# Weights stored as contiguous tiles, parameters in one pack, natural channel order, and the second gate's blocks moved into the mixers

## The chip, the cores and the metric

The kernel runs on one core of one Trainium2 chip. The metric is the device time of one execution in microseconds (us). Before the change three runs took 1486.04, 1483.69 and 1480.70 us, a median of 1483.69 us. A difference of about 0.3% (4.4 us) is what a measurement of this kernel can tell from no change.

## What is computed

A trunk of two layers over 256 tokens of 1024 channels in fp32, batch 1, with a conditioning vector c:

```python
cond = jax.nn.silu(c)
for l in range(DEPTH):
    mod = cond @ w_ada[l] + b_ada[l]
    shift1, scale1, gate1, shift2, scale2, gate2 = [m[:, None, :] for m in jnp.split(mod, 6, axis=-1)]
    h = rms_norm(x, norm1_g[l]) * (1 + scale1) + shift1
    proj = h @ w_in[l] + b_in[l]
    mq, mk, mv, mo, mgates, aq, ak, av, gm, ga = jnp.split(proj, offsets, axis=-1)
    y_m = mlstm_mixer(...)            # depthwise convolution of 5 taps on q and k, then a gated recurrence
    y_a = bidirectional_gqa(...)      # attention with q/k norms and rotary embedding
    merged = sigmoid(gm) * (y_m @ w_branch_m[l]) + sigmoid(ga) * (y_a @ w_branch_a[l])
    x = x + gate1 * (merged @ w_out[l])
    h2 = rms_norm(x, norm2_g[l]) * (1 + scale2) + shift2
    x = x + gate2 * hierarchical_moe(h2, ...)   # top group of 4, top 2 of its 8 experts, 32 experts of SwiGLU
return rms_norm(x, final_norm_g)
```

Nearly all the bytes are weights. Per layer `w_ada` has 25.2 MB, `w_in` 20 MB, `w_branch_m` and `w_branch_a` 2.1 MB each, `w_out` 4.2 MB, and the 32 experts 201.3 MB.

## The kernel before, in words

**One stream of weight tiles.** A list `plan` holds every weight tile in the order of use, a tile being 128 partitions of 2048 fp32 numbers, 1.049 MB. `pump()` (L156-173) walks through it: as long as a place is free that fits the next tile, SyncE (SP) issues its DMA (L172). `wt()` hands a tile to the arithmetic, and `done()` gives its place back. The places are 16 slots of an arena, of which 0, 1, 2 and 15 (`BASE`) always serve and the others only while their other contents are dead, three tiles "y", two tiles "x" (only while the experts run) and, in the mixer only, one tile "z" ("spare" in the profile). An expert tile never goes to "z". Since SP issues in the order of the plan, a tile that has no place holds back all that are behind it.

**The mixer** (`mixer`, one call per layer) computes everything up to `x + gate1 * ...`. Each weight tile is split on chip into a rounded part and a rest (`prep`, L532-547: a cast on ScalarE at L537, a subtraction at L518 on VectorE for one half and GpSimd for the other) and multiplied in three passes; a quarter of a 512-column pair of tiles is one `dense` step, 24 matmuls of TensorE (PE) that take about 3.1 us. The string `MIX[l]` is the order of the rest around these steps: a digit is a number of dense steps, a name is a piece of other work. `gates` and `gates2` make the recurrence's gates; `dec0` to `dec4` (L788-834) make its decays by short alternations of PE, VectorE and ScalarE; `r5` to `r9` and `r4` are blocks of 512 columns of the layer's own `w_ada`, `c0` to `c3` blocks of the next layer's. Each block has two tiles (`ada_sums`, L423-431), a round over ScalarE and VectorE (`ada_part`) and a pair of matmuls (`ada_sum`, "prow"). q and k go through the convolution in `fin_qk` (L605-615): one ScalarE copy with bias, one VectorE `tensor_scalar` (L611), four `scalar_tensor_tensor` (L613), one ScalarE silu.

**The end of the mixer.** After `MIX` come the two branch products, the output projection `wo` with `fin_wo` (L1094-1107), which writes x, the scaled copy `xa` (slot 5) and the same numbers in another channel order, `xaP` (slot 6), and the router's logits. The blocks 10 and 11 of `w_ada` (`GATES`, the second gate) stand in the plan behind `wo` and ahead of the experts' tiles. `ada_sums` of both runs on PE when the logits are done (L1153), and their sums are folded into `gt2b` in the first pair of experts (L1461-1463, L1482-1487, "prow").

**The experts** (`experts`) run 16 pairs. Per pair: 4 tiles of gate, 4 of up, 4 of down; the product act_mul (L1337), its transposes (L1343), their copy (L1344), the down product, and a scatter back into x. Behind pair 11 (`MIDDLE`) the program tests whether an expert has more than 64 rows (`rest`).

**Places at that moment.** When the second gate's blocks are on PE, the stream has the arena's 0, 1, 2, 15, then 8, 11, 12 (released at L1078) and 7, 13, 14 (`free:7:13:14` in `MIX`), and the three "y" (L1130): 13 places. The two "x" are released at the start of `experts` (L1169), and 4, 5 and 6 after the first one-hot (L1458): 18 in all.

**Weights in HBM** are the reference's arrays. A `w_ada`, `w_in`, `w_branch` or `w_out` tile is read in rows of 2 KB; an expert tile in rows of 8 KB, 16 KB apart. The small parameters come in some 20 DMAs: `params` (L317-351) reads rows that PE transposes (`params_cols`, L353-358), for layer 1 in its experts' pair 6; the router is read in both channel orders.

Of the kernel before, what the change touches and what calls it, by code (L numbers as in the profile page):

```python
# [54 lines left out]


def trunk(ctx, tc, x, c, w_ada, b_ada, norm1_g, w_in, b_in, conv_w, conv_b, mlstm_norm_g, q_norm_g, k_norm_g,
          w_branch_m, w_branch_a, w_out, norm2_g, w_rg, b_rg, w_re, b_re, w_gate, w_up, w_down, final_g,
          rope, out, dbg=None, depth=DEPTH):
# [183 lines left out]
    def first_params():  # L243
        first["p"] = params(0, nc.gpsimd, nc.sync)

    for l in range(depth):
# [5 lines left out]
        for it in stream(l):  # L252
            if it[0] in DENSE:
                o = DENSE[it[0]] + 512 * it[1]
                src = w_in[l].rearrange("(k p) c -> p k c", p=P)
# [1331 lines left out]
```

## Time and profile before

| what | us |
|---|---|
| median of three runs | 1483.69 |
| the profiled execution's own time | 1483.02 |
| its span, first to last instruction | 1481.1 |
| PE busy, of the span | 1345.1 (91%) |
| VectorE (DVE) busy | 630.1 (43%) |
| ScalarE (ACT) busy | 399.4 (27%) |
| GpSimd (POOL) busy | 281.2 (19%) |

521.5 MB move in the span. The profile's page gives the span in 40 slices of 37 us, with a row of the DMA rate in GB/s. The view of windows gives, for stretches of one's choice, each engine's busy time with its number of instructions, then the granted clock of PE as a share of full speed, the busy share of the 16 DMA engines (small overshoots over 1 are its rounding), and GB/s. The timeline gives start, duration, engine, line, operation, written and read tile and shape, and in brackets the idle time ahead of it with who ended it; on SP a row such as "x4" covers four issues with the waits between them. The mixer of layer 0 lies between 0 and 282 us, its experts between 282 and 757, the mixer of layer 1 up to 996, its experts up to the end.

### The profile page before, as it was taken

The numbers are of one execution on the slowest core, as the hardware profiler recorded it, in microseconds if no ns is written. First come the engines' busy times: TensorE is split into PE (matmuls) and PEld (weight loads), VectorE is DVE, ScalarE is ACT, GpSimd is POOL, SyncE is SP. The second block draws the span as 40 slices with busy tenths as digits, with TensorE's granted clock in tenths as the row PEclk, the third lists the DMA queues.
The fourth block names the chain that finished last, engine by engine and source line by source line (L and its number), as shares of the span: only waits on it lengthen the run. The fifth ranks groups of instructions, "written<-read, shape, count | busy, mean of one in ns | idle before, by whom it ended". The sixth has DMA issues, their size and how long they took to land. (4 is left out here: it accounts for less than half of the span.)

```text
span 1481.1 us, 20274 instructions
## 1 busy us (share of the span) xinstructions
PE 1345.1 (91%) x7870; PEld 782.3 (53%) x7871; DVE 630.1 (43%) x1390; ACT 399.4 (27%) x749; POOL 281.2 (19%) x321
## 2 busy tenths in 40 slices
PE   5899999899999989879889899998999989988996
PEld 2887789734434434234348788983443443434332
DVE  2786666613323313223258776664232332213223
ACT  2535564511101101001045367552110110101101
POOL 3645336300000000000025543550000000000000
PEclk8899999999999999999999999999999999999998
DMA  9956698699999999999997537659999999999995
GB/s 323 357 212 210 228 340 289 245 422 421 420 421 421 421 421 421 421 413 380 405 388 254 198 130 260 232 223 398 421 420 422 421 420 421 421 422 419 370 421 230
DMA packets 124248, 521.50 MB, mean 352 GB/s; under 512 B 15924, under 2 KB 18176, under 8 KB 76016
## 3 DMA queue, kind: packets, MB, share of 16 engines
q1 hardware_dynamic: 118064, 516.11, 87.7%
q0 software_dynamic: 1200, 2.13, 0.6%
q10 hardware_dynamic: 4880, 1.87, 0.5%
q8 instruction: 65, 1.06, 0.3%
q14 instruction: 39, 0.32, 0.1%
HBM read 519.03 MB, written 1.05 MB: 351 GB/s over the span
## 5 line engine op out<-in xcount | busy, mean ns | idle before, releaser
L1328 PE MATMUL pgu<-arena 128*64 128x512 f32 x1520 | 418.6, 594 | 17.7 <-DMA arena<-in_w_up_dram 14.0
L1328 PEld LDWEIGHTS pgu<-arena 128*64 128x64 f32 x1520 | 138.1, 137 | 235.7 <-issue 179.4
L1337 DVE SCALAR_TENSOR_TENSOR arena<-pgu,wsl,arena 128x512 f32<-128x512 f32 x32 | 36.4, 1136 | 391.8 <-PE pgu L1328 391.8
L1353 PE MATMUL pd<-arena 128*64 128x512 f32 x640 | 179.6, 601 | 10.8 <-ACT arena L1344 10.8
L1284 POOL TENSOR_TENSOR arena<-oh,arena 128x256 f32<-128x256 f32 x32 | 19.5, 615 | 733.0 <-DVE oh L1278 474.4
L596 PE MATMUL pd<-R,R 128*128 128x256 f32 x1056 | 139.7, 291 | 9.8 <-DVE R L518 5.5
L577 PE MATMUL pd<-R,R 128*128 128x256 f32 x1008 | 134.5, 292 | 8.3 <-ACT R L537 4.3
L596 PEld LDWEIGHTS pd<-R,R 128*128 128x128 f32 x1056 | 132.6, 196 | 14.9 <-DVE R L518 6.3
L577 PEld LDWEIGHTS pd<-R,R 128*128 128x128 f32 x1008 | 127.4, 197 | 17.2 <-ACT R L537 5.3
L1364 DVE TENSOR_TENSOR y<-pd,arena 128x512 f32<-128x512 f32 x64 | 44.1, 691 | 204.3 <-PE pd L1353 169.3
L518 POOL TENSOR_TENSOR R<-arena,R 128x512 fp32r<-128x512 f32 (+1 forms) x73 | 108.4, 1486 | 104.0 <-ACT R L537 80.3
L1328 PE MATMUL pgu<-X,arena 128*64 128x512 f32 x240 | 106.6, 594 | 6.4 <-DMA X<-in_w_up_dram 6.4
L1365 ACT CAST yh<-y 128x512 fp32r<-128x512 f32 x64 | 39.6, 619 | 241.7 <-DVE y L1364 241.7
L518 DVE TENSOR_TENSOR R<-arena,R 128x512 fp32r<-128x512 f32 (+1 forms) x81 | 75.8, 945 | 59.1 <-ACT R L537 49.7
L1353 PEld LDWEIGHTS pd<-arena 128*64 128x64 f32 x640 | 54.7, 138 | 87.1 <-issue 72.1
L1328 PE MATMUL pgu<-B,arena 128*64 128x512 f32 x288 | 87.1, 595 | 7.2 <-DMA B<-in_w_gate_dram 5.9
L1376 DVE TENSOR_TENSOR xs<-xs,psc 128x512 f32<-128x512 f32 x128 | 79.3, 679 | 19.0 <-PE psc L1373 19.0
L1300 PE MATMUL pG<-oh,X 128*128 128x256 f32 x512 | 70.6, 298 | 13.0 <-DVE oh L1278 12.0
L537 ACT CAST R<-arena 128x1024 fp32r<-128x1024 f32 x65 | 67.8, 1045 | 51.5 <-PE pd L596 15.5
L1300 PEld LDWEIGHTS pG<-oh,X 128*128 128x128 f32 x512 | 67.0, 204 | 24.1 <-issue 22.6
L1344 ACT COPY arena<-pat 128x512 f32<-128x512 f32 x32 | 18.7, 585 | 222.5 <-PE pat L1343 222.5
L1353 PE MATMUL pd<-B,arena 128*64 128x512 f32 x240 | 70.8, 595 | 3.6 <-ACT arena L1344 3.6
(346 smaller groups left out, 1708.9 us busy)
## 6 DMA issues: line engine op xcount, KB each, us to landing
arena<-in_w_up_dram SPq DMA_DIRECT2D x100, 1024.0 KB, 19.8
arena<-in_w_gate_dram SPq DMA_DIRECT2D x90, 1024.0 KB, 19.8
arena<-in_w_down_dram SPq DMA_DIRECT2D x80, 1024.0 KB, 19.8
arena<-in_w_ada_dram SPq DMA_DIRECT2D x35, 1024.0 KB, 7.7
B<-in_w_down_dram SPq DMA_DIRECT2D x30, 1024.0 KB, 19.8
arena<-in_w_in_dram SPq DMA_DIRECT2D x22, 1024.0 KB, 7.9
X<-in_w_gate_dram SPq DMA_DIRECT2D x20, 1024.0 KB, 19.8
B<-in_w_gate_dram SPq DMA_DIRECT2D x18, 1024.0 KB, 19.8
```

The lines of the kernel that those rows point to most:

```text
L518: eng.tensor_tensor(dst, full, hi.bitcast(F32), op=ALU.subtract)
L537: A.copy(wh, w)
L577: T.matmul(acc[key][o][:, 0:S], lhsT=w[:, kk, P * o:P * o + P], rhs=x_[:, 4 * kh + kk], start=kh == 0 and i == 0 and kk == 0, stop=kh == 1 ...
L596: T.matmul(acc[key][t][:, 0:256], lhsT=x_[:, 4 * kh + kk, P * t:P * t + P], rhs=w[:, kk], start=kh == 0 and i == 0 and kk == 0, stop=kh == ...
L1284: G.tensor_tensor(ow, oh[:, :, 2 * (i % 2):2 * (i % 2) + 2].bitcast(F32), cb[:, :, 2 * i:2 * i + 2].unsqueeze(3).to_broadcast([P, NT, 2, C ...
L1300: T.matmul(pG[:, kk, 0:n], lhsT=x_[:, t, k, :], rhs=oh[:, t, :], start=i == 0, stop=i == 3)
L1328: T.matmul(pg[CAP * e:CAP * e + CAP, :], lhsT=xg[4 * h + kk][:, P * (i % 2) + CAP * e:P * (i % 2) + CAP * e + CAP], rhs=w[e][:, kk, :], st ...
L1337: V.scalar_tensor_tensor(ac.rearrange("p k q -> p q k"), pu.rearrange("p (q k) -> p q k", k=4), wsl[:, 0:1], sl.rearrange("p (q k) -> p q ...
L1353: T.matmul(pd[n][CAP * e:CAP * e + CAP, :], lhsT=aT[:, 2 * h + kk, CAP * e:CAP * e + CAP], rhs=w[e][:, kk, 512 * n:512 * n + 512], start=h ...
L1364: V.tensor_tensor(y[:, cs], pd, gt2b[:, cs], op=ALU.mult)
L1365: A.copy(yh[:, cs], y[:, cs])
L1376: V.tensor_tensor(xx, xx, pq, op=ALU.add)
```

## The change

**Layouts.** The host writes each weight tile as one contiguous block of 1 MB (`ada_t`, `in_t`, `branch_t`, `out_t`, `gate_t`, `up_t`, `down_t`), so every tile is read in rows of 8 KB; only the last pair's down tiles stay at 2 KB. The small parameters of a layer are one array `packs[l]` of 128 x 540 numbers, already as columns, read by one DMA: for layer 0 on ScalarE's queue, for layer 1 on GpSimd's. The router is one array, read once per layer by GpSimd, in natural order.

**Natural channel order.** `xaP` and its eight copies per layer go; `experts` reads `xa`. Slot 6 is released with the "y" places instead of after the first one-hot. `shift_put` makes 4 matmuls instead of 8. act_mul writes a contiguous tile instead of one with a stride.

**Second gate.** `GATES` is gone: the blocks 10 and 11 are `r10` and `r11` in `MIX`, with `ada_part` and `ada_row` like the others, in both layers.

**Order.** In `MIX` the decays start behind the convolution: `dec0` stands six (layer 0) and six (layer 1) dense steps behind `gates2`. The convolution's first tap goes from VectorE to ScalarE.

```diff
-    "1 tables 1 gates 2 gates2 dec0 4 dec1 1 dec2 2 dec3 1 dec4 1 kr 2 1 kt qr:0 2 qr:1 r6 1 hold ...
+    "1 tables 1 gates 2 gates2 6 dec0 2 dec1 1 kr 1 dec2 1 dec3 r10 1 kt qr:0 1 dec4 1 qr:1 r6 1 hold ...
...
-            s = w_ada[l].rearrange("(p k) c -> p k c", k=KD)[:, 4 * h:4 * h + 4, 512 * b:512 * b + 512]
-            add(("ada", l, b, h), s, (4, 512))
+            add(("ada", l, b, h), ada_t[l, b, h].rearrange("p (k c) -> p k c", k=4), (4, 512))
...
-        for b in GATES:
-            plan_ada(l, b)
...
+    def params(l, q):
+        pk = sm.tile([P, NPK], F32, tag="pk", name="pk", bufs=1)
+        q.dma_start(pk, packs[l])
+        p = {nm: pk[:, o:o + n] for nm, (o, n) in PK.items()}
...
-            V.tensor_scalar(a, pre[:, 0:S], cols[:, 32 + j:33 + j], cols[:, 72 + j:73 + j], op0=ALU.mult, op1=ALU.add)
+            A.activation(a, pre[:, 0:S], AF.Identity, scale=cols[:, 32 + j:33 + j], bias=cols[:, 72 + j:73 + j])
...
-            dst = xaP[:, t, :, 32 * n:32 * n + 32].rearrange("p k q -> p q k")
-            if n == 3:
-                G.tensor_tensor(dst, xs[:, t, cs].rearrange("p (q k) -> p q k", k=KD),
-                                A2b[:, cs].rearrange("p (q k) -> p q k", k=KD), op=ALU.mult)
-            else:
-                A.copy(dst, xa[:, t, cs].rearrange("p (q k) -> p q k", k=KD))
...
-        release([("y", s) for s in range(3)])
+        release([("y", s) for s in range(3)] + [("a", 6)])
...
-        gates_ = [ada_sums(l, b) for b in GATES]
...
-            V.scalar_tensor_tensor(ac.rearrange("p k q -> p q k"), pu.rearrange("p (q k) -> p q k", k=4), wsl[:, 0:1],
-                                   sl.rearrange("p (q k) -> p q k", k=4), op0=ALU.mult, op1=ALU.mult)
+            V.scalar_tensor_tensor(ac.rearrange("p k q -> p (k q)"), pu, wsl[:, 0:1], sl, op0=ALU.mult, op1=ALU.mult)
...
-        release([("a", 4), ("a", 5), ("a", 6)])
+        release([("a", 4), ("a", 5)])
...
-                for h, s in enumerate(sums):
-                    pc = ps.tile([P, 512], F32, tag="f", name="prow")
-                    T.matmul(pc, lhsT=ones, rhs=s, start=True, stop=True)
...
-            if not last and i == 6:
-                params_cols(nextp)
```

**SP, the end of layer 0's mixer.** These are the DMAs from the output projection's weights on, before and then after; "B" are the "y" places and "X" the "x" places. Before:

```order
L172 DMA arena<-in_w_out_dram 128x4x512 x4
L172 DMA arena<-in_w_ada_dram 128x4x512 x4
L172 DMA arena<-in_w_gate_dram 128x2048 x2
L172 DMA B_2571<-in_w_gate_dram 128x2048
L172 DMA B_2572<-in_w_gate_dram 128x2048
L172 DMA B_2573<-in_w_up_dram 128x2048
L172 DMA arena<-in_w_up_dram 128x2048 x3
L172 DMA arena<-in_w_down_dram 128x2048 x4
L172 DMA arena<-in_w_gate_dram 128x2048
L172 DMA X_2929<-in_w_gate_dram 128x2048
```

After:

```order
L176 DMA arena<-in_out_t_dram 128x2048 x4
L176 DMA arena<-in_gate_t_dram 128x2048 x4
L176 DMA arena<-in_up_t_dram 128x2048 x2
L176 DMA B_2572<-in_up_t_dram 128x2048
L176 DMA B_2573<-in_up_t_dram 128x2048
L176 DMA B_2574<-in_down_t_dram 128x2048
L176 DMA arena<-in_down_t_dram 128x2048 x3
L176 DMA arena<-in_gate_t_dram 128x2048 x2
L176 DMA X_2901<-in_gate_t_dram 128x2048
```

The four blocks of `w_ada` between `wo` and the experts' tiles are gone, and 14 instead of 13 experts' tiles are issued ahead of the first "X", of which all 14 have a place that does not depend on the second gate's matmuls.

**VectorE, the output projection of layer 0.** "lc" is the router's offset, "R" the split weights, L1097 (L1046 after) the first operation of `fin_wo`. Before:

```order
L1136 TENSOR_TENSOR lc<-pL,br 128x36
L518 TENSOR_TENSOR R_146<-arena,R_146 128x512
L518 TENSOR_TENSOR R_145<-arena,R_144 128x256
L518 TENSOR_TENSOR R_147<-arena,R_147 128x512
L1097 TENSOR_TENSOR arena<-pd,arena 128x256 x2
```

After:

```order
L1079 TENSOR_TENSOR lc<-pL,pk 128x36
L471 TENSOR_TENSOR R_141<-arena,R_141 128x512
L471 TENSOR_TENSOR R_140<-arena,R_139 128x256
L471 TENSOR_TENSOR R_142<-arena,R_142 128x512
L696 TENSOR_TENSOR c1b<-c_726,pk 128x16
L665 SCALAR_TENSOR_TENSOR A_5315<-c1b,pk 128x8
L1046 TENSOR_TENSOR arena<-pd,arena 128x256 x2
```

Two small operations of layer 1 (its `c1` and `A1`, L696 and L665 of the changed kernel) now stand in the middle of layer 0's output projection. The first of them reads "pk", layer 1's pack, whose DMA GpSimd can issue only after "lc" has read layer 0's pack, since there is one buffer. Before, `c1` of layer 1 stood in the experts, behind the transposed parameters.

**PE, the end of layer 0's mixer.** "pL" are the logits, "pada" the blocks of `w_ada`, "pp" the routing's counts, "pG" the gather. Before:

```order
L1141 MATMUL pL<-arena 128x36 x4
L428 MATMUL pada<-arena,condp 32x512 x16
L1238 LDWEIGHTS trisb
L1238 MATMUL pp<-arena,trisb 128x64
L1239 LDWEIGHTS onesb
L1239 MATMUL pp<-arena,onesb 128x32
```

After:

```order
L1084 MATMUL pL<-arena 128x36 x4
L1180 LDWEIGHTS trisb
L1180 MATMUL pp<-arena,trisb 128x64
L1181 LDWEIGHTS onesb
L1181 MATMUL pp<-arena,onesb 128x32
```

The 16 matmuls of the second gate between the last logits and the counts are gone from this place and stand earlier, in two groups of 8 between dense steps.

More of the change, by code (lines that the diff above doesn't have):

```diff
@@ L243, in first_params @@
     def first_params():
-        first["p"] = params(0, nc.gpsimd, nc.sync)
+        first["p"] = params(0, nc.scalar)
     for l in range(depth):
@@ L445, in ada_fast, with columns @@
         return t
-    def ada_shift(l, b):
-        A.copy(turned_sums, ada_sums(l, b).rearrange("p (q k) -> p k q", k=KD))
-    def shift_put(sh2c, b3, b):
-        o = 64 * (b % 2)
-        pc = ps.tile([P, 512], F32, tag="f", name="pshift")
-        for k in range(KD):
-            T.matmul(pc[o:o + 64, 2 * k:2 * k + 2], lhsT=turned_sums[:, k, :], rhs=ones[:, 0:2], start=True, stop=True,
-                     tile_position=(0, o))
-        V.tensor_tensor(sh2c[o:o + 64, :], pc[o:o + 64, 0:2 * KD].rearrange("p (k o) -> p k o", o=2)[:, :, 0],
-                        b3[o:o + 64, :], op=ALU.add)
-    def ada_put(c1, cols, b, t):
+    def columns(t):
         pc = ps.tile([P, 512], F32, tag="f", name="pcol")
@@ L464, in ada_put, with ada_shift, shift_put @@
             T.matmul(pc[:, 2 * j:2 * j + 2], lhsT=t[:, P * j:P * j + P], rhs=ones[:, 0:2], start=True, stop=True)
-        V.tensor_tensor(c1[:, 4 * b:4 * b + 4], pc[:, 0:8].rearrange("p (j o) -> p j o", o=2)[:, :, 0],
-                        cols[:, 80 + 4 * b:84 + 4 * b], op=ALU.add)
+        return pc[:, 0:8].rearrange("p (j o) -> p j o", o=2)[:, :, 0]
+    def ada_shift(l, b):
+        A.copy(sums_at, ada_sums(l, b))
+    def shift_put(sh2c, b3, b):
+        s = slice(4 * (b % 2), 4 * (b % 2) + 4)
+        V.tensor_tensor(sh2c[:, s], columns(sums_at), b3[:, s], op=ALU.add)
+    def ada_put(c1, cols, b, t):
+        V.tensor_tensor(c1[:, 4 * b:4 * b + 4], columns(t), cols[:, 80 + 4 * b:84 + 4 * b], op=ALU.add)
     def ada_sum(parts):
@@ L1172, in experts @@
         pump()
-        xp = [t.rearrange("p (t k q) -> p t k q", t=NT, k=KD) for t in tiles["x"][2:4]]
+        xp = [t.rearrange("p (t c) -> p t c", t=NT) for t in tiles["x"][2:4]]
         used = [1024]
@@ L1455, in experts @@
         with tc.issue_after(marks["oh"].ins):
-            marks["lo"] = V.scalar_tensor_tensor(xp[1][:, 1], xaP[:, 1], r, xp[0][:, 1].bitcast(F32), op0=ALU.mult,
+            marks["lo"] = V.scalar_tensor_tensor(xp[1][:, 1], xa[:, 1], r, xp[0][:, 1].bitcast(F32), op0=ALU.mult,
                                                  op1=ALU.subtract)
-        release([("a", 4), ("a", 5), ("a", 6)])
+        release([("a", 4), ("a", 5)])
         gather(oh)
         urgent.close()
-        sums = [at(9, 512 * i, 512) for i in range(2)]
-        for s, pb in zip(sums, gates_):
-            A.copy(s, pb)
         with tc.issue_after(marks["lo"].ins):
```

157 lines of the change are left out of this document (71 added, 86 removed).

## The prediction

> **What bounds the kernel now.** I read the page's row of DMA rates first, since nearly all of the work is weights. Slices are 37 us.
>
> ```profile
> GB/s 323 357 212 210 228 340 289 245 422 421 420 421 421 421 421 421 421 413 380 405 388 254 198 130 260 232 223 398 421 420 422 421 420 421 421 422 419 370 421 230
> ```
>
> Two plateaus at 420 to 422 GB/s, the experts, and between them mixers at half of that. Two questions follow: does the stream or PE set the plateaus, and when do they begin? The view of windows (PE, PEld, DVE, ACT, POOL busy, then clock, DMA share, GB/s):
>
> ```profile
> 20.00:24.00 4.00, 3.20 (x28) 2.02 (x24) 1.85 (x7) 1.37 (x3) 1.39 (x3) 1.00 1.05 383
> 64.00:68.00 4.00, 4.00 (x21) 4.00 (x20) 1.02 (x2) 3.96 (x7) 1.78 (x1) 0.50 1.05 389
> 280.00:284.00 4.00, 3.24 (x30) 1.90 (x34) 3.79 (x21) 2.92 (x6) 0.89 (x1) 1.00 0.00 0
> 292.00:296.00 4.00, 4.00 (x25) 3.74 (x26) 2.29 (x11) 1.42 (x3) 0.00 (x0) 0.72 1.01 422
> 300.00:304.00 4.00, 4.00 (x17) 1.40 (x14) 0.14 (x1) 0.10 (x1) 0.00 (x0) 1.00 1.01 422
> 1000.00:1004.00 4.00, 2.94 (x28) 0.68 (x20) 3.36 (x20) 1.83 (x3) 0.00 (x0) 0.90 0.92 285
> 40.00:120.00 80.00, 71.47 (x544) 63.70 (x546) 62.19 (x158) 33.50 (x47) 44.92 (x60) 0.91 0.78 277
> 760.00:880.00 120.00, 108.34 (x852) 93.48 (x845) 92.49 (x237) 62.00 (x101) 62.45 (x71) 0.97 0.64 226
> ```
>
> At 280 the stream stands still; from 292 the DMA engines are full. An expert tile (1.049 MB) takes 1.049/0.422 = 2.49 us, a pair of 12 tiles 29.8 us. What PE needs for a pair is read from the copy that stands once in each pair (timeline of ScalarE):
>
> ```profile
> 313.90 0.58 ACT L1344 COPY arena<-pat 128x512 f32<-128x512 f32 x1 [8.11 <-PE pat L1343]
> ...
> 368.36 0.58 ACT L1344 COPY arena<-pat 128x512 f32<-128x512 f32 x1 [9.34 <-PE pat L1343]
> ...
> 421.11 0.58 ACT L1344 COPY arena<-pat 128x512 f32<-128x512 f32 x1 [9.34 <-PE pat L1343]
> ...
> 745.29 0.58 ACT L1344 COPY arena<-pat 128x512 f32<-128x512 f32 x1 [11.29 <-PE pat L1343]
> ...
> 1027.64 0.58 ACT L1344 COPY arena<-pat 128x512 f32<-128x512 f32 x1 [8.11 <-PE pat L1343]
> ```
>
> Two pairs took 421.11 - 368.36 = 52.75 us while tiles lay ready, 26.4 a pair. Fifteen took 745.29 - 313.90 = 431.4 where PE alone would need 396: some 35 us in which PE waited for tiles. So an experts' phase ends at the start of its full stream plus its remaining bytes, and tiles that have landed before the stream must wait are worth 2.49 us each. How many have landed is counted on SP's timeline:
>
> ```profile
> 231.93 10.98 SPq L172 DMA_DIRECT2D arena<-in_w_gate_dram  x2
> 249.03 0.80 SPq L172 DMA_DIRECT2D B<-in_w_gate_dram  x2
> 249.88 0.42 SPq L172 DMA_DIRECT2D B<-in_w_up_dram  x1
> 256.82 14.65 SPq L172 DMA_DIRECT2D arena<-in_w_up_dram  x3
> 273.58 11.70 SPq L172 DMA_DIRECT2D arena<-in_w_down_dram  x4
> ...
> 286.18 0.95 SPq L172 DMA_DIRECT2D X<-in_w_gate_dram  x2
> ```
>
> Of the last four-fold row the first went out at 273.58, the others had to wait until the second gate's tiles were read. So 2 + 2 + 1 + 3 + 1 = 9 tiles lay ready at 280, and the full stream runs from about 286. In layer 1 the window at 1000 moved 1.14 MB, 2.7 us at 422, so it starts near 1001.
>
> The mixers are another matter: in the two stretches from 40 and from 760 PE idles 8.5 and 11.7 us, VectorE is busy for 78%, and the clock (0.91, 0.97) costs PE another 6.4 and 3.3 us.
>
> **Start of layer 0.** Eight blocks of `w_ada` and x, 9.44 MB, must come ahead of the first dense step (PE's timeline):
>
> ```profile
> 30.31 1.93 PE L428 MATMUL pada<-arena,condp 128*32 128x512 f32 x8 [0.69 <-DMA arena<-in_w_ada_dram]
> ...
> 38.20 10.41 PE L577 MATMUL pd<-R,R 128*128 128x256 f32 x72 [2.45 <-ACT R L537]
> ```
>
> Up to 30.31 PE waits for a DMA. Rows of 2 KB went at 383 and 389 GB/s with the engines full, the experts' 8 KB rows at 422. After, 9.72 MB with the pack at 422 take 23.0 us, and with a head of 3 us (estimated: 9.44 MB at 383 would be 24.6, and the small loads stand between) the last tile lands at 26.0: -4.3. Bounds: the rate alone, 24.6 to 23.0, about -2; and -6 if the head goes with the small loads.
>
> By the Trainium skill ("DMA: Bandwidth & Descriptors", Specifications) a transfer is at line rate from 512 B on, so rows of 2 KB would lose nothing. The trace differs, 383 against 422 GB/s with full engines; by the page the term would be nil and the sum 1474.3.
>
> **Mixers.** Off VectorE goes the first tap, eight times in the stretch (groups of lines, mean ns behind the busy time):
>
> ```profile
> L611 DVE TENSOR_SCALAR arena<-arena,cols 128x256 f32<-128x256 f32 x8 | 3.2, 409 | 2.3 <-ACT arena L609 2.1
> ```
>
> That is 3.2 us a layer for an engine that PE waits for; ScalarE, which takes it, is busy for 42% of the stretch. The decays, short turns between three engines, leave the convolution's VectorE queue. Both together can take no more than the idle 8.5 and 11.7 us plus the clock's loss, and no less than nothing; I take -6 a layer, about twice the taps and half the idle time, a choice. Against that stand two rows r10 and r11 between dense steps. Their price (PE's timeline, first the 4 tiles of both blocks, then a pair of row sums):
>
> ```profile
> 282.10 3.64 PE L428 MATMUL pada<-arena,condp 128*32 128x512 f32 x32
> 287.78 0.20 PE L1238 MATMUL pp<-arena,trisb 128*128 128x64 bf16 x1 [2.04 <-DVE arena L1235]
> ...
> 290.52 5.23 PE L1300 MATMUL pG<-oh,X 128*128 128x256 f32 x29 [0.51 <-DVE X L1456]
> 295.68 3.65 PE L1328 MATMUL pgu<-arena 128*64 128x512 f32 x16
> ```
>
> ```profile
> 218.61 0.62 PE L471 MATMUL prow<-part,onesr 128*128 128x512 f32 x2
> ```
>
> 3.64 + 2 x 0.62 = +4.9 a layer, all of it on PE's path in the mixer. At the mixer's end it saves nothing: PE waited there for the routing (L1238 begins at 287.78 behind VectorE's L1235), and the 3.64 us lay in front of that. Net -1 a layer, -2 in all; bounds +10 (no relief) and -15. The copies `xaP` go from ScalarE and GpSimd, which did not end a wait there: zero.
>
> **PE cold at the end.** Without those matmuls PE is idle from 282.1 to 287.8, 5.7 us. The clock is already 0.72 in the window at 292, where the gather and the first gate matmuls run. I take +1 a layer, +2 in all; bounds nil, as it is low anyway, and +4, if the 5.23 us of the gather went at the 0.50 that the window at 64 shows instead of 0.72 (5.23 x 0.72/0.50 = 7.5).
>
> The Trainium skill ("TensorE: Matmul & The Clock Gate", Part 1) lets PE fall to half rate after an idle window of some 3.4 us; by that the gather would lose up to 1.7 us a layer and the sum would be 1.4 us more. The trace's 0.72, behind only 2.0 us of idle time, shows that the clock falls there without such a window too.
>
> **A new wait: layer 1's pack.** In VectorE's order `c1` of layer 1 (L696) now stands in layer 0's output projection. It needs layer 1's pack, which GpSimd can issue only after "lc", as there is one buffer. The nearest rows are the router's bias, which GpSimd issues at that place, and the two operations between which L696 would stand (timelines of GpSimd and VectorE, then DMA issues with KB and us to landing):
>
> ```profile
> 253.79 0.56 POOL L329 DMA_DIRECT2D br<-in_b_router_group_dram  x1
> ```
>
> ```profile
> 256.68 0.74 DVE L1097 TENSOR_TENSOR arena<-pd,arena 128x256 f32<-128x256 f32 x2
> 257.34 1.27 DVE L518 TENSOR_TENSOR R<-arena,R 128x512 fp32r<-128x512 f32 x1
> ```
>
> ```profile
> br<-in_b_router_group_dram POOLq DMA_DIRECT2D x1, 2.0 KB, 6.7
> br<-in_b_router_expert_dram POOLq DMA_DIRECT2D x1, 16.0 KB, 8.1
> ```
>
> So the pack (276 KB) lands between 253.8 + 6.7 = 260.5 and 262, and VectorE stands from 256.7 on. Behind L696 on its queue are `fin_wo`'s L1097 (L1046 now) and the split L518 (L471 now) of the next weights, which PE needs here:
>
> ```profile
> 260.81 3.11 PE L596 MATMUL pd<-R,R 128*128 128x256 f32 x24
> ```
>
> L518 would run from 261.2 to 262.7 or from 262.7 to 264.2 instead of ending at 258.6, with L1097 ahead of it. PE is late by 2 to 4 us, and the logits, which hang on `fin_wo`, by up to 5. I take +5, as the pack is 17 times the larger of the two loads; bounds +1 and +9. Layer 1 has no next pack.
>
> **Places of tiles.** After the change the second gate holds none of the arena's places at the mixer's end, and slot 6 serves earlier: 14 places, then the two "x" and slots 4 and 5, 18 in all. The first place comes back when the first gate half is done, 295.68 + 3.65 = 299.3, its new data some 2 us later, 301.5. By then 9 + (301.5 - 286) / 2.49 = 15.2 tiles have landed now, and 18 will have: a full ring, so the gain is 2.8 tiles, 7.0 us, and not the five tiles (12.4 us) of 14 against 9. In layer 1 the same point lies at 301.5 + (1027.64 - 313.90) = 1015.2, with 9.5 + 14.2 / 2.49 = 15.2 tiles landed (9 as in layer 0, and half a tile more by estimate, since what goes before 1001 isn't counted), and the gain is some 6.7 us. Together -13.7; bounds nil, if the mixer ends with places still unread, and -25.
>
> The rate in the experts' phases stays at 422: both kernels read those tiles in 8 KB rows. act_mul's straight tile lies under the stream: zero.
>
> **Sum.** -4.3 - 2 + 2 + 5 - 13.7 = -13.0, from the profiled execution's 1483.0 (0.7 under the median): **1470.0**.
>
> **Rivals.**
> *The relief is whole.* Both mixers lose all idle time (20.2) and half of the clock's loss (4.8), less 9.8 of added rows: -15.2 instead of -2, and the pack has landed in time: 1470.0 - 13.2 - 5 = 1451.8. For it speaks VectorE's 78%; against it that half of the idle time can have other causes.
> *Contiguous experts' tiles stream faster by 1%.* 945 us of stream in both layers make -9.4: 1460.6. Against it: the share is 1.01 already.
> *Rows of 2 KB were at line rate.* The start gives nothing: 1474.3, the page's rule from above.
> *The ring gains nothing.* The tiles ready are read no sooner, since the ring is full either way by the time PE takes the first: 1483.7.
> *The added rows wait for tiles (slower).* In the mixer r10 and r11 add four tiles to a stream that is busy for 78% from 40 to 120 and has few places there. If PE waits for both tiles of each of the four rows, 2 x 2.74 us at 383 GB/s, 22 us come on top: 1492. It decides from 4.4 us a row on (17.4 us in all); against it speaks that the blocks r5 to r9 come through that stretch already and VectorE, not the stream, is what is busiest beside PE there.
>
> **How the numbers follow.** Forecast 0.52, whole relief 0.14, faster stream 0.10, start without gain 0.08, ring without gain 0.09, waiting rows 0.07. About 0.3%, 4.4 us, is what a measurement of this kernel can tell from no change, so "same" is 1479.3 to 1488.1. The forecast's own terms scatter by some 7 us, so 0.05 of its 0.52 lies in it, with 0.06 of the full ring and 0.01 of the waiting rows: 0.12. Slower: 0.06 of the waiting rows and 0.01 of the full ring. Faster: 0.81. The range reaches from the whole relief, 1450, to the ring without gain, 1484.
>
> **What would show it.** Right: the DMA's first slice above 323 GB/s and dense steps from 34 on; no window at 0 GB/s ahead of the experts; a VectorE stall on "pk" in layer 0's output projection; copy L1344's successors 7 us earlier after the mixer's own shift; clock below 0.72 at the gather. Wrong: PE waiting on `w_ada` tiles between dense steps; stretches 40 to 120 and 760 to 880 with more PE idle time than 8.5 and 11.7; a plateau above 424 GB/s; "pk" landing before VectorE asks for it.

## The result, and the profile after

Six runs of the changed kernel took 1472.08 to 1475.85 us, median 1472.8, against 1485.09 for six of the kernel before: ratio 0.9927, interval 0.9911 to 0.9943, so 0.6 to 0.9% faster. The profiled execution took 1472.51 us, its span 1470.4, 10.7 less than before. The forecast was 1470.0, 13.0 less.

The page's row of DMA rates after, in slices of 37 us:

```profile
GB/s 383 368 257 238 253 366 276 205 367 419 419 420 419 420 420 419 420 393 399 413 411 258 241 175 233 233 261 294 420 419 419 420 419 419 420 419 418 372 420 236
```

The first slice has risen from 323 to 383. The slices at the start of the plateaus have fallen (367, and 294 in layer 1), which looks like a loss and isn't: there the ring, that is all the places for tiles, is full. And the plateau itself is at 419 to 420 where it was 421 to 422.

The first dense step (timeline of PE):

```profile
32.12 10.24 PE L530 MATMUL pd<-R,R 128*128 128x256 f32 x72 [2.45 <-ACT R L490]
```

It comes 6.1 us earlier than before (38.20). The last tile of `w_ada` that it needs is multiplied from 26.73 on where it was 30.31, 3.6 us earlier. The other 2.5 us lie behind that tile, where PE ran at a granted clock of 0.50 before and of 0.97 to 1.00 now: its 8 matmuls took 1.93 us and take 1.07, the 16 that follow took 3.57 and take 1.95 (before, then after; timeline and window of PE):

```profile
32.18 3.57 PE L464 MATMUL pcol<-onesr,arena 128*128 128x2 f32 x16
28.00:32.00 4.00, 3.31 (x16) 0.20 (x8) 0.00 (x0) 0.00 (x0) 0.00 (x0) 0.50 1.05 387
```

```profile
26.73 1.07 PE L385 MATMUL pada<-arena,condp 128*32 128x512 f32 x8 [0.57 <-DMA arena<-in_ada_t_dram]
27.73 1.95 PE L408 MATMUL pcol<-onesr,arena 128*128 128x2 f32 x16
28.00:32.00 4.00, 1.67 (x15) 1.59 (x15) 2.38 (x8) 1.85 (x4) 0.34 (x4) 0.97 1.00 410
```

The two mixers, each from its first dense step to the output projection, before and then after, in the view of windows:

```profile
38.20:250.53 212.33, 202.84 (x1606) 177.19 (x1607) 147.62 (x357) 113.81 (x211) 103.68 (x104) 0.96 0.77 271
766.26:965.75 199.49, 186.80 (x1504) 169.54 (x1501) 144.62 (x339) 110.98 (x208) 100.62 (x99) 0.98 0.65 226
```

```profile
32.12:244.54 212.42, 204.19 (x1627) 174.22 (x1627) 150.40 (x353) 119.72 (x223) 100.31 (x99) 0.98 0.74 288
756.26:959.59 203.33, 193.11 (x1525) 172.20 (x1521) 146.68 (x337) 117.39 (x221) 100.48 (x100) 0.97 0.63 242
```

Layer 0's is as long as it was; its PE has 1.4 us more of work, at a higher clock. Layer 1's is 3.8 us longer, with 6.3 us more work on PE and 2.5 us less idle time. The new wait in layer 0's output projection (timeline of VectorE, with what ended the idle time):

```profile
245.89 2.75 DVE L471 TENSOR_TENSOR R<-arena,R 128x512 fp32r<-128x512 f32 x3 [0.34 <-ACT R L490]
254.17 0.18 DVE L696 TENSOR_TENSOR c1b<-c,pk 128x16 f32<-128x16 f32 x1 [5.54 <-DMA pk<-in_packs_dram]
254.38 0.17 DVE L665 SCALAR_TENSOR_TENSOR A<-c1b,pk 128x8 f32<-128x8 f32 x1
254.47 0.75 DVE L1046 TENSOR_TENSOR arena<-pd,arena 128x256 f32<-128x256 f32 x2
255.14 0.68 DVE L471 TENSOR_TENSOR R<-arena,R 128x512 fp32r<-128x512 f32 x1
```

VectorE stands for 5.5 us in front of `c1`, and the split of the next weights, L471, is queued behind it. PE feels it a moment later, and then loses its work at the mixer's end:

```profile
244.74 8.67 PE L549 MATMUL pd<-R,R 128*128 128x256 f32 x71
257.12 1.38 PE L1058 MATMUL pxa<-ident,arena 128*128 128x128 f32 x4 [3.71 <-POOL arena L1049]
...
279.63 0.86 PE L1084 MATMUL pL<-arena 128*128 128x36 f32 x6 [0.32 <-ACT arena L1059]
285.97 0.23 PE L1180 MATMUL pp<-arena,trisb 128*128 128x64 bf16 x1 [5.48 <-DVE arena L1177]
...
287.64 5.89 PE L1242 MATMUL pG<-oh,X 128*128 128x256 f32 x32 [1.36 <-DVE oh L1220]
```

The stretch from the output projection's first matmul to the last logits takes 280.5 - 244.5 = 36.0 us, 4.3 more than the 31.6 of before. Windows around the experts' start show the ring filling up:

```profile
284.00:288.00 4.00, 0.67 (x6) 0.60 (x7) 3.32 (x13) 0.00 (x0) 0.00 (x0) 0.50 0.57 240
288.00:292.00 4.00, 3.88 (x21) 3.59 (x21) 2.23 (x10) 0.78 (x3) 0.00 (x0) 0.60 0.47 174
292.00:296.00 4.00, 4.00 (x25) 2.25 (x26) 2.65 (x10) 2.71 (x4) 1.19 (x2) 1.00 0.22 92
296.00:300.00 4.00, 4.00 (x22) 1.29 (x18) 0.00 (x0) 0.00 (x0) 0.00 (x0) 1.00 0.47 125
300.00:304.00 4.00, 4.00 (x22) 1.35 (x20) 0.76 (x2) 0.60 (x1) 0.62 (x1) 1.00 1.01 424
```

From 288 to 300 the rate is 174, 92 and 125 GB/s. In windows of 1 us the stream all but stands from 287 to 290 (0 to 16 GB/s) with 17 tiles asked for, reads the eighteenth, which SP issues at 288.76, and stands from 293 to 298, when PE has freed the first place. Before, it ran at 422 there. From the first gate matmul to the last copy the stream moved less than before in both layers (windows, before and then after):

```profile
295.68:745.29 449.61, 413.65 (x1950) 172.78 (x1949) 124.19 (x212) 52.08 (x93) 12.36 (x23) 0.99 1.01 415
1009.42:1458.35 448.93, 412.96 (x1949) 172.92 (x1948) 123.91 (x209) 52.01 (x93) 9.76 (x16) 1.00 1.00 416
```

```profile
293.47:735.79 442.32, 408.78 (x1945) 171.27 (x1944) 117.63 (x205) 52.20 (x92) 10.74 (x22) 0.99 0.99 410
1005.34:1447.87 442.53, 409.90 (x1945) 170.22 (x1944) 117.54 (x204) 51.99 (x93) 9.78 (x16) 0.99 0.99 410
```

That is 187 MB before and 181 after, five tiles fewer. The copies that stand once in each pair, layer 1's last before and then the first and last of each layer after:

```profile
1458.35 0.58 ACT L1344 COPY arena<-pat 128x512 f32<-128x512 f32 x1 [11.32 <-PE pat L1343]
```

```profile
309.58 0.59 ACT L1285 COPY arena<-pat 128x512 f32<-128x512 f32 x1 [8.35 <-PE pat L1284]
...
735.79 0.59 ACT L1285 COPY arena<-pat 128x512 f32<-128x512 f32 x1 [10.96 <-PE pat L1284]
...
1021.46 0.59 ACT L1285 COPY arena<-pat 128x512 f32<-128x512 f32 x1 [8.36 <-PE pat L1284]
...
1447.87 0.59 ACT L1285 COPY arena<-pat 128x512 f32<-128x512 f32 x1 [10.96 <-PE pat L1284]
```

Read as shifts against before: 4.3 us at layer 0's first pair, 9.5 at its last, 6.2 at layer 1's first, 10.5 at its last. So by layer 1's first pair 3.3 us of what layer 0 won are given back; layer 1's mixer takes 3.8 us more and its gather 2.0.

| stretch of the profiled execution | before | after | change | forecast |
|---|---|---|---|---|
| start to first dense step | 38.2 | 32.1 | -6.1 | -4.3 |
| mixer 0 to output projection | 212.3 | 212.4 | +0.1 | -1 |
| output projection 0 to last logits | 31.6 | 36.0 | +4.3 | +5 |
| routing and gather 0 | 13.5 | 13.0 | -0.5 | +1 |
| first gate matmul to last copy, 0 | 449.6 | 442.3 | -7.3 | -7.0 |
| to layer 1's first dense step | 21.0 | 20.5 | -0.5 | 0 |
| mixer 1 to output projection | 199.5 | 203.3 | +3.8 | -1 |
| output projection 1 | 31.7 | 31.7 | 0 | 0 |
| routing and gather 1 | 12.0 | 14.1 | +2.0 | +1 |
| first gate matmul to last copy, 1 | 448.9 | 442.5 | -6.4 | -6.7 |
| tail | 22.8 | 22.5 | -0.2 | 0 |

### The profile page after: what moved, and what is told of

It is laid out like the page before. It is cut to its first block, busy times and chain, and to the rows that moved or that the text cites. A ratio compares the mean times of both kernels' runs of the same rounds, so it can differ in the third digit from the quotient of the medians.

```text
span 1470.4 us, 20138 instructions
## 1 busy us (share of the span) xinstructions
PE 1336.9 (91%) x7836; PEld 777.5 (53%) x7837; DVE 617.7 (42%) x1376; ACT 403.3 (27%) x755; POOL 263.5 (18%) x295
## 5 line engine op out<-in xcount | busy, mean ns | idle before, releaser
L1270 PE MATMUL pgu<-arena 128*64 128x512 f32 x1504 | 376.0, 595 | 21.1 <-DMA arena<-in_up_t_dram 13.0
L1270 PEld LDWEIGHTS pgu<-arena 128*64 128x64 f32 x1504 | 121.6, 137 | 246.7 <-issue 193.7
L1279 DVE SCALAR_TENSOR_TENSOR arena<-pgu,wsl,arena 128x512 f32<-128x512 f32 x32 | 24.0, 751 | 389.4 <-PE pgu L1270 389.4
L1294 PE MATMUL pd<-arena 128*64 128x512 f32 x680 | 160.3, 594 | 7.3 <-ACT arena L1285 7.3
L549 PE MATMUL pd<-R,R 128*128 128x256 f32 x1056 | 137.7, 289 | 3.3 <-DVE arena L589 1.7
L471 POOL TENSOR_TENSOR R<-arena,R 128x512 fp32r<-128x512 f32 (+1 forms) x74 | 112.9, 1528 | 147.4 <-ACT R L490 113.2
L549 PEld LDWEIGHTS pd<-R,R 128*128 128x128 f32 x1056 | 131.4, 195 | 10.7 <-issue 6.7
L530 PE MATMUL pd<-R,R 128*128 128x256 f32 x1008 | 132.1, 289 | 4.7 <-ACT R L490 3.6
L1270 PE MATMUL pgu<-B,arena 128*64 128x512 f32 x384 | 116.2, 594 | 4.1 <-DMA B<-in_up_t_dram 2.7
L1294 PEld LDWEIGHTS pd<-arena 128*64 128x64 f32 x680 | 50.2, 137 | 95.3 <-issue 85.6
L471 DVE TENSOR_TENSOR R<-arena,R 128x512 fp32r<-128x512 f32 (+1 forms) x82 | 73.8, 909 | 55.8 <-ACT R L490 49.3
L1246 ACT ACTIVATE arena<-pG,sh2c 128x256 f32<-128x256 f32 x64 | 30.4, 475 | 156.1 <-DVE arena L1248 156.1
L1278 ACT ACTIVATE arena<-pgu 128x512 f32<-128x512 f32 x32 | 19.1, 597 | 189.7 <-PE pgu L1270 189.7
```

What stands on the lines that cost most here:

```text
L471: eng.tensor_tensor(dst, full, hi.bitcast(F32), op=ALU.subtract)
L530: T.matmul(acc[key][o][:, 0:S], lhsT=w[:, kk, P * o:P * o + P], rhs=x_[:, 4 * kh + kk], start=kh == 0 and i == 0 and kk == 0, stop=kh == 1 ...
L549: T.matmul(acc[key][t][:, 0:256], lhsT=x_[:, 4 * kh + kk, P * t:P * t + P], rhs=w[:, kk], start=kh == 0 and i == 0 and kk == 0, stop=kh == ...
L1246: A.activation(xg[k][:, 0:n], pG[:, kk, 0:n], AF.Identity, bias=sh2c[:, k:k + 1])
L1270: T.matmul(pg[CAP * e:CAP * e + CAP, :], lhsT=xg[4 * h + kk][:, P * (i % 2) + CAP * e:P * (i % 2) + CAP * e + CAP], rhs=w[e][:, kk, :], st ...
L1279: V.scalar_tensor_tensor(ac.rearrange("p k q -> p (k q)"), pu, wsl[:, 0:1], sl, op0=ALU.mult, op1=ALU.mult)
```

## The experiments

The changed kernel is undone in one part each time. Of several executions of the same order of instructions, layer 1's mixer agrees within 0.8 us (202.6 to 203.4), layer 0's lies at 212.4 to 213.1 or, in e8 and e11, at 215.1 to 215.2, so that one profile settles less than 3 us there. Medians are of the timed runs, ratios against the kernel before on the same chip.

**Layer 1's pack is asked for later (e1).**

```diff
-            V.tensor_tensor(c1, mods[l], cols[:, 80:96], op=ALU.add)
+            with tc.issue_after(p["after"]): V.tensor_tensor(c1, mods[l], cols[:, 80:96], op=ALU.add)
...
-                nextp = params(l + 1, nc.gpsimd)
+                nextp = dict(params(l + 1, nc.gpsimd), after=marks["lo"].ins)
```

> Only two small VectorE operations of layer 1 (c1 and A1) move, behind layer 0's first one-hot. Theory (the wait for layer 1's pack costs layer 0): VectorE's stall of 5.5 us in layer 0's output projection is gone, the projection takes 31.6 us instead of 35.8 on PE as before the change, the first gate matmul and the full stream come 4.1 us earlier, and the end 3 to 4.5 us earlier: 1468 to 1470 against 1472.8. Rival (hidden: the ring is full anyway, so an earlier end of the mixer buys nothing): the stall is gone, the end moves by less than 1 us.

Median 1470.83, ratio 0.9927 (0.9913 to 0.9941). The stall is gone (VectorE), and layer 0's last copy (ScalarE) comes 3.5 us earlier than the 735.79 of the changed kernel:

```profile
246.15 2.73 DVE L471 TENSOR_TENSOR R<-arena,R 128x512 fp32r<-128x512 f32 x3 [0.35 <-ACT R L490]
250.38 0.91 DVE L1046 TENSOR_TENSOR arena<-pd,arena 128x256 f32<-128x256 f32 x2 [1.50 <-PE pd L549]
```

```profile
732.30 0.58 ACT L1285 COPY arena<-pat 128x512 f32<-128x512 f32 x1 [10.98 <-PE pat L1284]
```

The projection took 31.6 us again, as the theory has it; the stretch to the last copy kept 3.5 of the 4.1 us, and the span 2.2, since layer 1's first dense step came only 2.0 us earlier. There PE's clock was 0.79 in the 8 us from 744 where the changed kernel had 1.00 at the same place (744 to 756). The medians, 12.7 under before against 12.3, don't tell 2 us from nothing. So the wait and its price within layer 0 are shown; that it costs the whole kernel as much is not shown.

**The second gate at the mixer's end again (e2).**

```diff
+        for b in GATES:
+            plan_ada(l, b)
...
+        gates_ = [ada_sums(l, b) for b in GATES]
```

The names r10 and r11 leave `MIX`, and the folding of the sums into the first pair comes back.

> The second gate's blocks stand at the mixer's end again, as before the change; all else stays changed. Theory (the places of the four tiles are worth some 5.6 to 7 us a layer, and the two added rows cost 3 to 5 us of PE in each mixer): mixers 3 to 5 us shorter each, 9 or 10 expert tiles instead of 18 landed when PE reads the first, the stream some 7 us later in relation to the first gate matmul; the end 4 to 10 us later, 1477 to 1483. Rival (the ring gains nothing): the end comes 6 to 10 us earlier, 1463 to 1467.

Median 1472.52, ratio 0.9933: no difference, which neither side expected. The mixers:

```profile
31.95:243.67 211.72, 202.61 (x1590) 176.57 (x1591) 144.47 (x349) 118.51 (x221) 102.06 (x99) 0.96 0.69 269
761.14:958.64 197.50, 186.15 (x1489) 170.86 (x1485) 142.19 (x333) 116.30 (x219) 102.70 (x100) 0.97 0.60 228
```

In layer 0 the rows cost 0.7 us (212.4 against 211.7), with PE's clock at 0.98 with them and 0.96 without; that is less than the 2.8 us by which this mixer scatters, so their price there is not settled. In layer 1 they cost 5.8 (203.3 against 197.5). From the first gate matmul to the last copy the move gains 4.1 us in layer 0 (446.5 against 442.3) and 1.7 in layer 1 (444.3 against 442.5). So of the 7.3 and 6.4 us that these stretches are shorter than before, 3.2 and 4.6 came without it. What brought them is not shown: with the blocks at the end, slot 6 still gives a place earlier, and 10 and 11 tiles had been asked for when SP stopped to wait, 9 and 10 in the kernel before, but no run takes slot 6 out of this version. With what lies between, layer 0's last copy comes 4.9 us later with the blocks at the end (740.68), and layer 1, from its first dense step to its last copy, is 4.9 us shorter. In these profiles the move wins in one layer what it loses in the other.

**Experts' tiles interleaved again (e3).**

```diff
-transpose(0, 1, 2, 4, 3, 5), (L, NE, 2, P, SLOT))
+transpose(0, 1, 4, 2, 3, 5), (L, NE, P, 2, SLOT))
```

> The experts' tiles lie in memory as before the change, two tiles interleaved, rows of 8 KB that are 16 KB apart; channel order and everything else as changed. Theory (the changed plateau of 419 to 420 GB/s instead of 421 to 422 has nothing to do with the layout): plateau 419 to 420, 1472.8 within 2 us. Rival (contiguous tiles stream slower by 0.4%): plateau 421 to 422, some 945 us of stream by 0.4% are 4 us, 1469. Second rival (contiguous streams faster and something else slows it): plateau under 418, 1476 or more.

Median 1474.93, ratio 0.9948 (0.9936 to 0.9960), with every stretch within 0.3 us of the changed kernel's and the plateau at 419 to 420. The experts' layout neither gains anything nor explains the lower plateau.

**Rows of 2 KB in the mixers (e4).**

```diff
-            add(("ada", l, b, h), ada_t[l, b, h].rearrange("p (k c) -> p k c", k=4), (4, 512))
+            add(("ada", l, b, h), ada_t[l].rearrange("(p k) c -> p k c", k=KD)[:, 4 * h:4 * h + 4, 512 * b:512 * b + 512], (4, 512))
```

and likewise for the other three weights.

> The tiles of w_ada, w_in, w_branch and w_out are read in rows of 2 KB from the reference's arrays again; packs, experts' tiles and order stay changed. Theory (rows of 2 KB cost 8 to 9% of the rate where the stream sets the pace): the first 37 us slice falls from 383 to some 350 GB/s, dense steps begin at 34 to 36 instead of 32.1, the end 2 to 4 us later: 1475 to 1477. Rival (rows of 2 KB are at line rate, and the 6.1 us of the start came from the 20 small loads that are gone): dense at 32.1, 1472.8.

Median 1479.12, ratio 0.9974 (0.9964 to 0.9984): all of the gain is lost but 0.3%. The first dense step falls back to 37.15. Windows ahead of it, of this kernel and then of the changed one:

```profile
16.00:20.00 4.00, 4.00 (x32) 2.57 (x31) 0.42 (x1) 0.00 (x0) 0.00 (x0) 1.00 1.04 386
20.00:24.00 4.00, 3.22 (x32) 2.17 (x32) 1.98 (x7) 1.50 (x4) 0.00 (x0) 0.99 1.05 388
28.00:32.00 4.00, 3.33 (x16) 1.07 (x13) 0.00 (x0) 0.59 (x1) 0.21 (x2) 0.50 1.05 384
```

```profile
16.00:20.00 4.00, 3.58 (x18) 1.53 (x20) 1.26 (x9) 0.00 (x0) 0.00 (x0) 0.50 1.03 425
20.00:24.00 4.00, 4.00 (x32) 2.15 (x28) 0.61 (x4) 0.59 (x1) 0.00 (x0) 0.81 1.00 416
```

With the engines full, rows of 2 KB move 386 to 388 GB/s and rows of 8 KB 416 to 425. Here the rows of 2 KB also lie apart in memory, not one behind the other; the experiment before this one has rows of 8 KB that are 16 KB apart, at no loss, but rows of 2 KB packed closely were not run. Of the start's 6.1 us the rows are 5.0, more than the rates alone explain (9.7 MB make 25.1 against 23.0 us). The rest is PE's clock: the last tile is multiplied 2.5 us later than in the changed kernel (29.26 against 26.73), and behind it PE runs at 0.50 (28 to 32) where that one has 0.97, which makes 2.5 more. The remaining 1.1 us of the 6.1 came with the other parts of the change, presumably with the small loads, which no run takes alone. So the rule of the Trainium skill ("DMA: Bandwidth & Descriptors", Specifications) that a transfer is at line rate from 512 B on does not hold for these tiles: 386 against 420 GB/s.

**The decays early again, with r10 and r11 in place (e5).**

```diff
-gates2 6 dec0 2 dec1 1 kr 1 dec2 1 dec3 r10 1 kt qr:0 1 dec4 1 qr:1 r6
+gates2 dec0 4 dec1 1 dec2 2 dec3 1 dec4 1 kr 2 r10 1 kt qr:0 2 qr:1 r6
```

This is layer 1's string; layer 0's goes back likewise, with its r11 and r10 in place.

> The decays stand right behind gates2 again, as before the change; r10 and r11 stay in the mixers, all else stays changed. Theory (moving the decays was worth little: the time before and after it differ by 0.6 us in layer 0 and 2 us in layer 1 once the added rows are taken out): the stretch from the first dense step to the output projection takes 212.4 to 214 us in layer 0 instead of 212.4, and 203.3 to 206 in layer 1 instead of 203.3; end within 3 us of 1472.8. Rival (the relief that was forecast, 6 us a layer): 217 and 208, end 5 to 9 us later, 1478 to 1482.

Median 1479.14, ratio 0.9976 (0.9964 to 0.9987): the rival was right on the whole. Layer 1's mixer takes 208.1 us, 4.8 more, as PE's idle time grows from 10.2 to 16.0; layer 0's 2.1 more, which is within its scatter:

```profile
31.97:246.47 214.50, 204.64 (x1627) 175.37 (x1627) 151.77 (x353) 119.80 (x223) 100.37 (x99) 0.99 0.74 285
758.39:966.48 208.09, 192.11 (x1524) 171.22 (x1521) 148.04 (x337) 117.91 (x221) 102.46 (x100) 0.98 0.62 237
```

PE's waits in layer 1's mixer show the new one, a row sum behind VectorE's part of it, L395 (0.2 us in the changed kernel):

```profile
PE prow L424 <- DVE part L395: 3.9, 2, 3.7
```

Without the added rows the old order cost next to nothing: layer 1's mixer takes 198.0 us with it in e9 below, and 197.5 with the new order and the tap moved in e2. With them it costs 4.8.

**The first tap on VectorE (e6).**

```diff
-            A.activation(a, pre[:, 0:S], AF.Identity, scale=cols[:, 32 + j:33 + j], bias=cols[:, 72 + j:73 + j])
+            V.tensor_scalar(a, pre[:, 0:S], cols[:, 32 + j:33 + j], cols[:, 72 + j:73 + j], op0=ALU.mult, op1=ALU.add)
```

> The convolution's first tap is on VectorE again, eight operations of 0.41 us a layer. Theory (VectorE's queue is not what holds PE in that stretch now): both mixers within 1 us, end within 1.5 us of 1472.8. Rival (they lie on the path): 2 to 3.3 us more in each mixer, end at 1477 to 1479.

Median 1476.57, ratio 0.9957 (0.9944 to 0.9971); layer 1's mixer 204.1, 0.7 more, layer 0's 213.7, within its scatter. The span is 1.9 us longer, the median 3.8. That lies between the two expectations. The interval just misses the changed kernel's (up to 0.9943), so the tap is worth a little, and the runs leave open how much, up to some 4 us.

**PE kept busy at the mixer's end (e7).**

```diff
+        hot = ps.tile([P, 512], F32, tag="f", name="hot")
+        for _ in range(4):
+            T.matmul(hot, lhsT=ident, rhs=g1b[:, 0:512], start=True, stop=True)
```

> Four matmuls with no use, 128x512 in fp32, some 4 us, stand between the last logits and the routing's counts, where PE is idle for 5.5 us. Theory (the idle time makes the clock fall at the gather): the gather takes 4.8 us in both layers instead of 5.8 and 7.0, the first gate matmul comes 1 and 2.2 us earlier, the end 2 to 3 us earlier, 1470. Rival (the clock falls for another reason): gather unchanged, end within 1 us.

Median 1473.67, ratio 0.9940: no gain that the times show. Gather of layer 1 in the changed kernel and here (PE):

```profile
998.34 7.07 PE L1242 MATMUL pG<-oh,X 128*128 128x256 f32 x32 [1.37 <-DVE oh L1220]
```

```profile
998.82 0.59 PE L1245 MATMUL pG<-oh,X 128*128 128x256 f32 x3 [1.36 <-DVE oh L1223]
999.92 3.73 PE L1245 MATMUL pG<-oh,X 128*128 128x256 f32 x29 [0.51 <-DVE X L1401]
1003.58 1.94 PE L1273 MATMUL pgu<-arena 128*64 128x512 f32 x8
```

In layer 1 the theory holds: from the gather's start to the first gate matmul 4.8 us instead of 7.0. In layer 0 it took 5.9 as in the changed kernel, but there the added matmuls did not fill the gap (PE in layer 0, then the windows of both gathers, layer 0 first):

```profile
280.70 3.68 PE L1098 MATMUL hot<-arena,ident 128*128 128x512 f32 x8
286.35 0.20 PE L1183 MATMUL pp<-arena,trisb 128*128 128x64 bf16 x1 [1.97 <-DVE arena L1180]
287.98 0.70 PE L1245 MATMUL pG<-oh,X 128*128 128x256 f32 x3 [1.37 <-DVE oh L1223]
```

```profile
288.00:292.00 4.00, 3.59 (x17) 3.29 (x18) 2.00 (x7) 0.78 (x3) 0.00 (x0) 0.57 0.50 137
1000.00:1004.00 4.00, 4.00 (x31) 3.64 (x33) 2.89 (x15) 1.71 (x5) 0.00 (x0) 1.00 0.69 252
```

They ended at 284.4, and until the gather at 288.0, 3.6 us, PE worked for only 0.3 us. In layer 1 they took 5.3 us, at a clock that fell to 0.50 in between, and ended 1.9 us ahead of the gather. The other runs fall in line. In the kernel before such a stretch ahead of the gather is 3.7 us in layer 0 and 2.0 in layer 1, and the gather takes 6.3 and 4.8; in e2 it is 3.5 in both layers, and the gather takes 6.3 in both. So the idle time fits both layers, and four matmuls were too few to show it in layer 0. The Trainium skill ("TensorE: Matmul & The Clock Gate", Part 1) has PE at half rate after an idle window of some 3.4 us: the gathers agree, slow behind 3.5 us and more with next to no work, fast behind 2.0. Elsewhere less was enough: in the kernel before, PE idled from 60.2 to 62.8, 2.6 us, and its clock was at 0.50 from 62.25 on.

**Slot 6 late again (e8).**

```diff
-        release([("y", s) for s in range(3)] + [("a", 6)])
+        release([("y", s) for s in range(3)])
...
-        release([("a", 4), ("a", 5)])
+        release([("a", 4), ("a", 5), ("a", 6)])
```

> Slot 6 is released after the first one-hot again, as before the change, so 13 instead of 14 tiles have a place ahead of the experts. Theory (full ring: what counts is how many tiles have landed when PE frees the first place, 18 either way): the stream still fills the ring before the first release, end within 1 us of 1472.8. Rival (each tile ahead is worth 2.5 us): the time from the first gate matmul to the last pair's copy grows by 2.5 us in each layer, end at 1477 to 1478.

Median 1474.72, ratio 0.9940. From the first gate matmul to the last copy 442.35 and 442.50 us, in the changed kernel 442.32 and 442.53: nothing. A place more ahead of the experts is worth nothing when the ring fills up anyway; the span's 2.6 us more lie in layer 0's mixer, on its other level.

**The mixers' tiles alone, in the kernel before (e9).** Its edit is the layout lines of e4 the other way round, in the kernel before.

> One part of the change alone: the kernel before, with the tiles of w_ada, w_in, w_branch and w_out as contiguous blocks; experts' tiles, small loads, order and places as before. Theory (the 5 us that rows of 2 KB cost at the start are a part that stands by itself): dense steps begin at 33 instead of 38.2, and the end comes 5 to 6 us earlier, 1478 against 1483.5. Rival (they only count with the rest of the change): within 2 us of 1483.5. Beside it the plateau: 421 to 422 GB/s if the changed kernel's 419 to 420 came with the change, 419 to 420 if it came with the chip that it ran on.

Median 1481.08, ratio 0.9985 (0.9974 to 0.9996). The start is 5.0 us shorter (33.15), but the times give only 0.05 to 0.4%, 1 to 4 us, less than the theory, and not clear of the rival's 2 us; its runs reach from 1476.1 to 1484.1. Layer 1's mixer takes 198.0 us, 1.5 less than before. The plateau is 420 to 422 on the chip on which the next experiment shows 419 to 420, so the lower plateau comes with the change.

**The gate's blocks by layer, and the pack late (e10).** MIX[0] as changed; GATES = ((), (10, 11)), so that layer 1 has its blocks at the end, as in e2; and the edit of e1.

> The changed kernel with two edits: c1 and A1 of layer 1 behind layer 0's first one-hot, and the second gate's blocks at the mixer's end in layer 1 only (r10 and r11 stay in layer 0's mixer). Theory (the moved blocks gain 4.9 us in layer 0, where the mixer gives their time back by the clock, and lose 4.9 us in layer 1, and the pack's wait is 2 to 3.5 us): layer 1 from its first dense step to the last pair's copy takes 687 us instead of 691.6, the whole 1464 to 1467. Rival (the gains of layer 1 don't add to those of layer 0): 1469 to 1471, no faster than with the pack's wait alone taken away.

Median 1466.58, ratio 0.9886 (0.9871 to 0.9902), clear of the changed kernel's 0.9911 to 0.9943 and of e1's 0.9913 to 0.9941: the gain of layer 1 adds. From layer 1's first dense step, 752.96, to this copy:

```profile
1440.14 0.59 ACT L1289 COPY arena<-pat 128x512 f32<-128x512 f32 x1 [10.99 <-PE pat L1288]
```

that is 687.2 us, against 691.6, as expected. This is the fastest version here.

**The plateau (e11, e12).** e11 only changes the order in which the arrays are declared; e12 gives act_mul its old stride, and so computes another product.

```diff
-    return {**experts, "ada_t": whole(ada, (L, 12, 2, P, SLOT)),
+    return {"ada_t": whole(ada, (L, 12, 2, P, SLOT)),
...
-            "packs": whole(packs, (L, P, NPK)), "router": whole(router, (L, P, 288))}
+            "packs": whole(packs, (L, P, NPK)), "router": whole(router, (L, P, 288)), **experts}
```

> The changed kernel with its arrays declared in another order: the experts' tiles behind the mixers' tiles, packs and router, as the experts' weights stood behind the mixers' before the change. No instruction changes. Theory (the experts' stream is 0.3 to 0.4% slower than before because of where its arrays lie in memory): windows in the experts show 421 instead of 419 to 420 GB/s, and the end comes 2 to 3 us earlier. Rival (where they lie has no part in it): 419 to 420, end as the changed kernel's within its scatter of 1472 to 1476.

```diff
-            V.scalar_tensor_tensor(ac.rearrange("p k q -> p (k q)"), pu, wsl[:, 0:1], sl, op0=ALU.mult, op1=ALU.mult)
+            V.scalar_tensor_tensor(ac.rearrange("p k q -> p q k"), pu.rearrange("p (q k) -> p q k", k=4), wsl[:, 0:1], sl.rearrange("p (q k) -> p q k", k=4), op0=ALU.mult, op1=ALU.mult)
```

> The changed kernel, with act_mul reading and writing in the stride that it had before the change; the product's channels are then in another order than the down weights', so this computes something else in the experts. Theory (the straight tile lies under the stream and costs or gains nothing there): act_mul takes 1.1 us instead of 0.75, plateau 419 to 420, the end 0 to 0.8 us later. Rival (VectorE's straight writes get in the way of the stream's): plateau 421, the end 2 us earlier.

Single runs of 1474.94 and 1474.41; the plateau stays at 419 to 420 in both. Neither place nor stride alone is the cause.

## Why the prediction was right

Direction and size were right, and most of the places; the sum was 13.0 and the spans differ by 10.7. That the sum came so close is luck in part: the mixers missed by 5.9 us, and the start, the routing of layer 0, the output projection and smaller stretches made up 3.6 of it on balance.

- **Start**: the step was right, -6.1 against -4.3, but it left out the clock. The last tile comes 3.6 us earlier, where 4.3 were forecast (the "eight blocks" of the prediction are eight tiles; its 9.44 MB are right); another 2.5 us come from PE's clock, 0.97 instead of 0.50 behind that tile. The rows of 2 KB alone cost 5.0 (e4), half of it by that clock.
- **Places of tiles**: -7.3 and -6.4 against -7.0 and -6.7, and by the mechanism: the ring fills up, and the stream stands until the first place comes free. Five tiles fewer were left to read, 12.4 us; against them stand some 5 us without a stream in layer 0 and 1.7 us of the lower rate, which leaves 5.7 of the 7.3. Two things in it were not as forecast. Layer 1 had 10 tiles ready before, not 9 (SP issued two of the down tiles by 988.79, the third at 999.30), so the prediction's own rule would have given some 4.5 us there, and that 6.7 came so close is luck. And only 4.1 and 1.7 us came from moving the second gate (e2); the rest came with something else in the change, and slot 6, worth nothing beside the move (e8), was not tried without it. The sign "no window at 0 GB/s ahead of the experts" was badly chosen: a full ring makes such windows.
- **New wait**: 5.5 us on VectorE and 4.3 on PE's path, against 5; the pack landed 6.5 us after GpSimd issued it (247.7 to 254.2), like the router's bias of before (6.7). Taking it away shortened layer 0 by 3.5 us (e1), the whole span by 2.2, which the medians don't tell from nothing.
- **Mixers**: this step failed. Net -1 a layer was forecast, +0.1 and +3.8 were measured. The prediction took relief and added rows as terms that add. The runs show for layer 1 that they don't: the decays' move is worth 4.8 us with the rows there (e5), while all of the relief without the rows is 2.0 (199.5 before against 197.5 in e2), and 1.5 of that came with contiguous tiles alone (198.0 in e9), so that 0.5 is left of the 6 forecast, less than the scatter. The rows' price, 4.9 by PE's own time, was 5.8 in layer 1 (e2). In layer 0 it was 0.7, within the scatter; whether the clock gave it back there is not shown.
- **PE cold**: +2.0 in layer 1 against +1, shown by e7 to come from the idle time; nothing in layer 0, where the clock was low before and stays so. The prediction saw 2.0 us of idle time ahead of that clock and concluded that it falls without a longer one. The 2.0 us end at four small matmuls, 0.3 us of work, and 1.4 us more follow: 3.7 us in all, so that row does not show it.
- **Rate of the experts**: "stays at 422" was wrong by 0.4%. Some 440 us of stream a layer make 1.7 us each. Layout (e3), chip (e9 with e10), place in memory (e11) and act_mul's stride (e12) are each excluded; the cause stays open.

Of the rivals, the added rows as a slower case had the right place, but not the way: in neither mixer of the changed kernel did PE wait for a tile of `w_ada`. The whole relief, the faster stream (419 to 420 GB/s, not above 422), the ring without gain and the 2 KB rows at line rate are refuted.

## What to carry to other kernels

Price a prefetch by what has landed when the first place comes free, not by the places it opens. An edit that suits one layer can cost as much in the next: test it by layer before it is kept, since a sum of nothing may hide 4.9 us each way. When small loads become one pack with one buffer, its DMA waits for the last reader of the pack before it, and every early reader of the new one waits with it; so look at which queue stands behind the first operation that reads the next layer's pack. When a filler is to keep PE busy, check on the timeline that it reaches up to the work it is meant for.

## What was not expected of the hardware

With all 16 DMA engines full, rows of 2 KB moved 386 to 388 GB/s and rows of 8 KB 416 to 425 (e4 and the changed kernel). With the same order of instructions layer 0's mixer took 212.4 us in one execution and 215.2 in another. And waits cost PE more than their length: a gather of 4.8 us took 5.8 to 7.0 behind 3.5 to 7.2 us with 0.3 us of work in them, and late tiles at the start cost 2.5 us of waiting and 2.5 us of a clock of 0.50.
